# The last MLP block's first product in Strassen form, its weight sums made by accumulating loads, with a plain product at the seam ahead of it

## The chip, the core and the metric

The kernel runs on one core of a Trainium2 chip. The metric is device time in microseconds (us) of one execution; the median of three runs is given with their extremes. A separate execution was recorded by the profiler, and all readings of the trace come from that one.

The names used below are those of the profile: PE is TensorE (matrix products, PEld its weight loads), DVE is VectorE, ACT is ScalarE, POOL is GpSimd, SP is SyncE, which issues most DMAs.

## The reference, cut to what matters

One layer of a hybrid decoder: forgetting attention and an mLSTM side by side, an output projection with layer norm, then an MLP. The change touches only the MLP, which works on 2048 prompt tokens and 64 sampled ones:

```python
x1 = _layer_norm(DN_ALPHA * x + mix, ln1_g, ln1_b)
hid = jnp.square(jax.nn.relu(x1 @ w1))        # w1: 1024 x 4096
return _layer_norm(DN_ALPHA * x1 + hid @ w2, ln2_g, ln2_b)   # w2: 4096 x 1024
```

All is float32. A product is made on PE from parts: an operand is split into a high part, in a shorter format (fp32r in the profile), and a low part (the rest), and three products stand for one: high·high, high·low, low·high.

## The kernel before

The last phase, `phase_c`, goes through the tokens in four blocks (`CB`): three of 512 tokens, and a fourth of 512 prompt tokens with the 64 sampled ones, so W = 576. In a block the 4096 hidden units are cut into eight steps `p` of 512. Step p makes its hidden values in two halves (`hidden(p, half)`, 256 units each) and then adds their part of the second product (`output(p, …)`) to the rows `ys` of the tokens. The steps are staggered: the first half of step p + 1 is issued ahead of `output(p)`, the second half behind it.

`hidden` loads two pieces of w1 (128 x 1024 values, 512 KB each) into tiles `wr` (`raw`, five buffers), splits each into `wh` on ACT (`split_hi`, L153) and `wl` on DVE (`split_lo`, L156; `piece`, four buffers of each), and multiplies: for 2 groups `f` of 128 units, 2 stretches of 288 tokens and 8 pieces `k` of the sum over 1024, three matmuls each (`mm3`, L162 to L164) on the turned x, `x1h` and `x1l`. Each result leaves its PSUM tile `ph` by ACT, as relu (L1460) and square (L1461), into `hq`.

`output` is already in Strassen's form with Winograd's additions: seven products, in the order `order`, in place of eight (84 matmuls of 512 columns in place of 96), each of sums of `hq` (tile `s`, L1508) and of sums of w2, which were made ahead in DRAM (`dw2`, by `w2_sum`, L1224, on POOL's queue). Its results leave their PSUM tiles `py` by DVE (`add`, L1478). The sampled tokens take a product of their own on both halves of PE (`two_sides`, L169). The last step of the fourth block is a plain product, `plain(7)`.

The turned x of a block is made during the last step of the block before: `x1_load` brings a tile of 128 tokens into `xr` (`landing`, two buffers), `x1_turn` transposes it on PE into a tile `px` or `px2` (L1286) and splits it. During the second and third steps of a block the layer norm of the block before (`normed`, L174 to L183) is called piece by piece from the list `later`. In the third block the sampled attention, which fills gaps through the whole phase (`tick`), comes to its end in step 5; it uses four tiles `S` of 128 x 1024 for its scores and the ring `kT`, which afterwards takes the loads of w2 in the fourth block (`spare`).

The program is written for a scheduler: it lays each engine's instructions in one fixed order, and an engine runs its queue in that order, each instruction waiting for the semaphores it names. `tc.issue_after` holds a load back behind an instruction named. Memory is given out by pools with a fixed number of buffers, so a load also waits until the last reader of its buffer is done.

## Time and profile before

| what | us |
|---|---|
| median of three runs | 3163.31 (3162.18 to 3174.97) |
| the profiled execution | 3159.55 |
| its span in the trace | 3157.6 |
| PE busy in the span | 3088.5 |
| DVE, ACT, POOL busy | 2080.6, 1436.6, 911.5 |

The profiled execution lies 3.8 us below the median. The span is the time from the first to the last instruction of that execution; the sum of the prediction is set against 3159.55. Engines overlap, so their busy times are not to be added. The page names releasers and groups by line numbers of the kernel printed above. The fourth block runs from about 2750 us to the end of the span; the lines on it are read in the prediction.

### The profile page before, as it was taken

To read this page: it belongs to the slowest core of one execution; us is meant where nothing else is said; L and a number is where in the kernel's file an instruction comes from. 1 tells how busy PE (TensorE), PEld (TensorE's weight loads), DVE (VectorE), ACT (ScalarE), POOL (GpSimd) and SP (SyncE) were. 2 spreads that over 40 slices of the span, in tenths; PEclk is the share of its full clock that TensorE was granted. 3 is DMA by queue.
4 is the path that set the end of the run, shared out by engine and by line. 5 is a ranking of instruction groups with operands and counts; after the bars stand their busy time and mean duration, and the time that the engine had idled before them with its cause. 6 is when DMAs were issued, how large, how long until landed. Compare 5 with 4: busy or idle time off the path is not lost.

```text
span 3157.6 us, 53760 instructions
## 1 busy us (share of the span) xinstructions
PE 3088.5 (98%) x19869; PEld 2442.9 (77%) x19869; DVE 2080.6 (66%) x5025; ACT 1436.6 (45%) x2629; POOL 911.5 (29%) x976
## 2 busy tenths in 40 slices
PE   8999999999999999999999999999999999999998
PEld 8997787787766667777777776776777777898886
DVE  6956557465488888544566577665586656867667
ACT  4343244334377777422445444453454443554442
POOL 0121232333433433376333324223334121000000
PEclk9999999999999999999999999999999999999999
DMA  5565675877787865587987878868788766543331
GB/s 191 155 213 180 228 234 189 284 269 243 234 260 202 209 172 134 212 304 261 330 289 280 309 255 335 318 242 315 290 308 328 289 230 215 183 154 141 104 118 64
DMA packets 323294, 731.80 MB, mean 232 GB/s; under 512 B 63032, under 2 KB 153656, under 8 KB 322136
## 3 DMA queue, kind: packets, MB, share of 16 engines
q1 hardware_dynamic: 235688, 412.83, 39.5%
q0 software_dynamic: 83808, 304.91, 27.3%
q10 hardware_dynamic: 3536, 10.62, 0.9%
q8 instruction: 157, 2.57, 0.3%
q14 instruction: 105, 0.86, 0.1%
HBM read 675.67 MB, written 86.12 MB: 241 GB/s over the span
## 4 chain that ended last, share of the span: by engine, by line
PE 84%; DMA 6%; DVE 4%; issue 2%; ACT 2%; POOL 1%; SPq 0%; DVEq 0%; POOLq 0%; ACTq 0%
PE ph L164 7%; PE ph L162 7%; PE ph L163 7%; PE py L162 6%; PE py L164 6%; PE py L163 6%; PE pm L162 6%; PE pm L164 6%; PE pm L163 6%; PE sO L1965 3%; PE po L1090 3%; PE sQ L1852 3%; PE pt L1080 3%; DMA vt<-cache_v,idxV 3%; PE pS L1035 2%
## 5 line engine op out<-in xcount | busy, mean ns | idle before, releaser
L156 DVE TENSOR_TENSOR wl<-wr,wh 128x1024 fp32r<-128x1024 f32 x300 | 365.7, 1221 | 227.9 <-ACT wh L153 226.9
L153 ACT ACTIVATE wh<-wr 128x1024 fp32r<-128x1024 f32 x300 | 315.6, 1055 | 323.3 <-PE ph L163 152.9
L1829 POOL DMA_INDIRECT kT<-cache_k,idxK x256 | 276.4, 1080 | 625.4 <-PE sQ L1852 560.9
L163 PE MATMUL ph<-x1l,wh 128*128 128x512 f32 (+1 forms) x1280 | 452.1, 353 | 1.8 <-DVE x1l L156 1.8
L162 PE MATMUL ph<-x1h,wh 128*128 128x512 f32 (+1 forms) x1280 | 453.4, 355 | 0.3 <-ACT x1h L153 0.3
L164 PE MATMUL ph<-x1h,wl 128*128 128x512 f32 (+1 forms) x1280 | 449.2, 354 | 0.2
L162 PE MATMUL py<-wh,hh 128*128 128x512 f32 x900 | 354.3, 399 | 0.3 <-ACT hh L153 0.2
L163 PE MATMUL py<-wl,hh 128*128 128x512 f32 x900 | 352.3, 393 | 0.0
L164 PE MATMUL py<-wh,hl 128*128 128x512 f32 x900 | 350.4, 393 | 1.6 <-DVE hl L156 1.6
L1478 DVE TENSOR_TENSOR y<-y,py 128x512 f32<-128x512 f32 x410 | 276.1, 681 | 109.7 <-PE py L164 107.2
L1941 POOL DMA_INDIRECT vt<-cache_v,idxV x197 | 209.8, 1065 | 347.9 <-PE sO L1965 272.3
L162 PEld LDWEIGHTS ph<-x1h,wh 128*128 128x128 f32 x1280 | 240.6, 188 | 36.8 <-issue 6.1
L164 PEld LDWEIGHTS ph<-x1h,wl 128*128 128x128 f32 x1280 | 239.9, 188 | 37.3 <-issue 4.5
L163 PEld LDWEIGHTS ph<-x1l,wh 128*128 128x128 f32 x1280 | 240.5, 188 | 36.3 <-issue 3.7
L162 PE MATMUL pm<-xh,whi 128*128 128x512 f32 (+2 forms) x640 | 230.7, 360 | 0.0
L164 PE MATMUL pm<-xh,wlo 128*128 128x512 f32 (+2 forms) x640 | 228.2, 357 | 0.0
L163 PE MATMUL pm<-xl,whi 128*128 128x512 f32 (+2 forms) x640 | 227.3, 355 | 0.0
L162 PE MATMUL pm<-whi,xh 128*128 128x256 f32 (+4 forms) x624 | 202.8, 326 | 8.6 <-ACT whi L153 8.6
L156 DVE TENSOR_TENSOR wlo<-wra,whi 128x1024 fp32r<-128x1024 f32 (+1 forms) x112 | 140.3, 1254 | 105.4 <-ACT whi L153 105.0
L162 PEld LDWEIGHTS py<-wh,hh 128*128 128x128 f32 x900 | 168.8, 189 | 46.8 <-issue 11.8
L164 PEld LDWEIGHTS py<-wh,hl 128*128 128x128 f32 x900 | 169.5, 188 | 41.0 <-issue 3.3
L163 PE MATMUL pm<-wlo,xh 128*128 128x256 f32 (+4 forms) x624 | 200.7, 322 | 0.6 <-DVE wlo L156 0.6
(380 smaller groups left out, 6476.4 us busy)
## 6 DMA issues: line engine op xcount, KB each, us to landing
wr<-w SPq DMA_DIRECT2D x200, 512.0 KB
wra<-w_in SPq DMA_DIRECT2D x104, 512.0 KB
wr<-dw SPq DMA_DIRECT2D x96, 512.0 KB
dw<-w POOLq DMA_DIRECT2D x48, 512.0 KB, 7.6
Rb<-dR SPq DMA_DIRECT2D x128, 128.0 KB
kT<-dw SPq DMA_DIRECT2D x28, 512.0 KB
kT<-w SPq DMA_DIRECT2D x25, 512.0 KB
xn<-xp_t SPq DMA_DIRECT2D x16, 512.0 KB
```

What stands on the lines that cost most here:

```text
L153: last["ACT"] = A.activation(dst, src, AF.Copy, scale=scale)
L156: r = (eng or V).tensor_tensor(dst, src, hi.bitcast(F32), op=OP.subtract)
L162: T.matmul(ps, wh, xh, start=first, stop=False, skip_group_check=shared)
L163: T.matmul(ps, wh, xl, start=False, stop=False, skip_group_check=shared)
L164: last["PE"] = T.matmul(ps, wl, xh, start=False, stop=stop, skip_group_check=shared)
L1080: turned = T.transpose(pt[:, k], sc[i][0][k0 // 8][:, c:c + 128], ident)
L1090: last["PE"] = T.matmul(po[c:c + 64, q0:], z["vn"][:, k], PTs[k // 4][:, k % 4, q0:], start=(k < 2), stop=(k >= nk - 2), skip_group_check= ...
L1478: V.tensor_tensor(y, y, ps, op=op)
L1829: G.indirect_dma_start(out=piece(n), out_offset=None, in_=ck, in_offset=IO(ap=idxK[:, b, j // 2, j % 2:j % 2 + 1], axis=0))
L1852: r = T.matmul(pq[h4 * 32:h4 * 32 + 32, hg].rearrange("p (k c) -> p k c", k=2), z["qb"][:, hd], kv, start=(db == 0), stop=(db == 1), skip_ ...
L1941: vx["last"] = G.indirect_dma_start(out=vt.rearrange("p f c -> p (f c)"), out_offset=None, in_=cv, in_offset=IO(ap=idxV[:, b, (kt % 4) * 4 ...
L1965: after_ = T.matmul(po[r:r + 32], z["PT"][:, hg, 2 * f + g, pg].rearrange("p h q -> p (h q)"), vts[f][:, g, hg * 256:(hg + 1) * 256], star ...
```

## The change

The fourth block's first product takes the form that the second one has. With x1 cut into four quarters (two halves of the tokens, two of the sum over 1024) and w1 likewise, seven products `n` of sums give the four quarters of the result. `hidden_s(p, …)` makes a step's 512 units at once, in the order `H_ORDER` = 1, 6, 7, 4, 5, 3, 2: for each product 2 groups f, 4 pieces k and three matmuls of 288 columns, so 7 x 2 x 4 x 3 = 168 matmuls a step, where there were 192.

The seven operands of x are made once. `last_block` loads the block's four row tiles into memory that the sampled attention has left (`nat`); `operand_sums` makes the sums on POOL, during step 6 of the third block; `operand_turn` transposes and splits each of seven operands of two tiles, and `sampled_turn` does the same for the sampled rows. These turns are spread over the output products of steps 6 and 7 of the third block, in PSUM tiles `side` that the sampled attention has left.

The operands of w1 are made anew in each step, by loads. Four loads bring quarters into tiles for the products 1, 6, 7 and 5, and one each later for 3 and 2; accumulating loads (`more`, on POOL's queue) add a second quarter to 7 and 5, and a second and a third to 6. When the tile of product 6 has been split, a fourth quarter is added to it, and it is split again as product 4's operand. A step so has six plain loads and five accumulating ones of w1, where it had four plain ones. Seven pieces are split where there were four. The signs are taken by the results: ACT copies the results of products 1, 6 and 7 into `hq` tiles (L1599 of the changed kernel), DVE adds or subtracts those of 5, 3 and 2 (L1604), ACT makes relu and square.

At the seam the third block's last second product is plain (`plain`, 96 matmuls of 512 columns for 84), with the turns of the last four operands between its products, and the third block's layer norm is done in two pieces a tile on DVE (`in_two`), with g and b in the memory of `nat`. The four tiles `S` become one tile `S4`, and the two buffers of `xr` one tile of double size; in the fourth block both hold hidden values, operands and the sampled rows' hidden values, which POOL gathers (`gather_sampled`). The loads of w2 in the fourth block take five slots: three of the attention's tiles (`wx`) and, from step 0 on, two of `nat`'s.

Steps are staggered as before, with a difference at the start: `hidden_s(0)` and `hidden_s(1)` stand one behind the other, then `output(0)`, `hidden_s(2)`, `output(1)` and so on; the end is `output(6)` and `plain(7)`.

The core of the diff (`-` before, `+` after):

```diff
-    kx = dict(ring=None, new=False, free=False)
+    kx = dict(ring=None, new=False, free=False, S=ps_.tile([128, 4096], F32, name="S4"))
...
+        xo, nat, diff = {}, {}, kx["S"][:, 1152:2688].rearrange("p (i c) -> p i c", i=3)
+        def last_block():
+            slots.extend([ps_.tile([128, 1024], F32, name="wx", tag=t, bufs=b) for t, b in (("vt", 2), ("vt", 2), ("PTs", 1))])
+            nat[12], nat[13], nat[14], nat[15] = kx["S"][:, 0:1024], slots[0], kx["S"][:, 2688:3712], slots[1]
+            for t in (12, 14, 13, 15):
+                SY.dma_start(nat[t], dx1[t * 128:t * 128 + 128])
+            x = pk_.tile([128, 5, 4, 288], F32R, name="xo5", tag="kT", bufs=1)
+            for i, n in enumerate((5, 6)):
+                xo[n] = [x[:, i * 2], x[:, i * 2 + 1]]
+            xo[3] = [x[:, 4], pcw.tile([128, 4, 288], F32R, name="xo1", tag="xr", bufs=1)]
...
+        def operand_sums(j):
+            xa, xb = nat[12 + j], nat[14 + j]
+            G.tensor_tensor(diff[:, 0], xb[:, 0:512], xb[:, 512:1024], op=OP.subtract)
+            G.tensor_tensor(xb[:, 0:512], xa[:, 0:512], xb[:, 0:512], op=OP.subtract)
+            G.tensor_tensor(diff[:, 1], diff[:, 0], xa[:, 0:512], op=OP.subtract)
+            G.tensor_tensor(diff[:, 2], xa[:, 512:1024], diff[:, 1], op=OP.add)
...
+        def operand_turn(n, j):
+            if n not in xo:
+                x1_pool()
+                x = C["px"].tile([128, 4, 2, 4, 288], F32R, name="xo")
+                for i, m in enumerate((1, 7, 2, 4)):
+                    xo[m] = [x[:, i, 0], x[:, i, 1]]
+            xa, xb = nat[12 + j], nat[14 + j]
+            src = {1: xa[:, 0:512], 2: xa[:, 512:1024], 4: xb[:, 512:1024], 7: xb[:, 0:512],
+                   5: diff[:, 0], 6: diff[:, 1], 3: diff[:, 2]}
+            px = side_bank().rearrange("p (k c) -> p k c", k=4)
+            for k in range(4):
+                T.transpose(px[:, k], src[n][:, k * 128:k * 128 + 128], ident)
+            h, l = (x[:, :, j * 128:j * 128 + 128] for x in xo[n])
+            split_hi(h, px)
+            C["turned"] = split_lo(l, px, h)
...
+            def h_tile():
+                count[0] += 1
+                if ci == 3 and count[0] % 4 == 0:
+                    return kx["S"][:, 1152:2304].rearrange("p (f c) -> p f c", f=2)
+                return ph.tile([128, 2, 576], F32, name="hq", bufs=3)
...
+            def hidden_ops(p):
+                w = lambda q: I["w1"][q % 2 * 8 + p, q // 2]
+                R = {}
+                def load(n, q):
+                    R[n] = raw()
+                    SY.dma_start(R[n], w(q))
+                def more(n, q):
+                    with tc.issue_after(last["POOL"].ins):
+                        last["POOL"] = G.dma_start(R[n], w(q), accum_op=OP.add)
+                for n in (1, 6, 7, 5):
+                    load(n, 0 if n != 7 else 3)
+                for n in (6, 7, 5):
+                    more(n, 1)
+                more(6, 3)
+                load(3, 3)
+                def made(n):
+                    r = piece(None, R[6 if n == 4 else n].rearrange("p (k c) -> p k c", k=4))
+                    if n == 1:
+                        load(2, 2)
+                    elif n == 6:
+                        more(6, 2)
+                    return r
+                return made, {}
+            H_ORDER = (1, 6, 7, 4, 5, 3, 2)
...
+                X = [ppc.tile([128, 512], F32, name="ph", tag="ph", bufs=2)[:, 0:288] for _ in range(2)]
+                Z = None
+                for at_, n in enumerate(H_ORDER):
+                    hidden_made(hp, H_ORDER[:at_ + 3])
+                    wh, wl = hp[1][n]
+                    xh, xl = xo[n]
+                    if n in (5, 2):
+                        Z = [side_bank()[:, 0:288] for _ in range(2)]
+                    for f in range(2):
+                        ps = (X if n in (1, 6, 7, 4) else Z)[f]
+                        c = slice(f * 128, f * 128 + 128)
+                        for k in range(4):
+                            mm3(ps, wh[:, k, c], wl[:, k, c], xh[:, k], xl[:, k], n in (1, 5, 2) and k == 0, n in (4, 3, 2) and k == 3, True)
+                        if n in (1, 6, 7):
+                            A.copy(part({1: 0, 6: 1, 7: 3}[n], f), ps)
+                        elif n == 4:
+                            A.activation(part(2, f), ps, AF.Relu)
+                        else:
+                            o = part({5: 3, 3: 1, 2: 0}[n], f)
+                            V.tensor_tensor(o, ps, o, op=OP.add if n == 2 else OP.subtract)
+                        if f == 1 and n in (4, 5, 3, 2):
+                            o = whole({4: 2, 5: 3, 3: 1, 2: 0}[n])
+                            if n != 4:
+                                A.activation(o, o, AF.Relu)
+                            A.activation(o, o, AF.Square)
+                    if n == 2:
+                        gather_sampled(p)
+                    if later:
+                        later.pop(0)()
+                    hooks.pop(at_, lambda: None)()
...
+            if ci == 3:
+                hp = {0: C.pop("hs")}
+                def begin(p):
+                    hp[p] = hidden_ops(p)
+                ops_of = lambda p, *ns: lambda: pre.append(ahead(p, *ns))
+                pre = []
+                hidden_s(0, hp.pop(0), {5: lambda: begin(1), 6: lambda: hidden_made(hp[1])})
+                for p in range(7):
+                    hidden_s(p + 1, hp.pop(p + 1), {5: lambda: begin(p + 2) if p < 6 else None, 6: ops_of(p, *order[:2])})
+                    if p == 0:
+                        slots.extend(C["gb"])
+                    output(p, pre.pop(), [], {5: early if p == 6 else lambda: hidden_made(hp[p + 2])})
+                plain(7, [(i, half) for i in range(4) for half in range(2)], [], {})
+                break
...
+                elif p == 6 and ci == 2:
+                    operand_sums(0)
+                    for n in (5, 6, 3):
+                        turns += [lambda: None, lambda: None, lambda: None, lambda n=n: operand_turn(n, 0)]
+                    turns.append(lambda: operand_sums(1))
+                elif p == 7:
+                    turns = [lambda n=n, j=j: operand_turn(n, j) for n in (1, 7, 4, 2) for j in range(2)]
+                    turns.insert(2, sampled_turn)
...
+                    if p == 7 and ci == 2:
+                        plain(p, [(i, half) for half in range(2) for i in range(4)], turns,
+                              {4: lambda: hidden_made(C["hs"], H_ORDER[:1]), 6: lambda: hidden_made(C["hs"])})
+                        while turns:
+                            turns.pop(0)()
+                    else:
+                        output(p, pre[0], turns, {})
```

Three places show how the order of instructions moves. A row names line, operation, output and inputs with the shape, and behind it the semaphores that it waits for. First PE, in a step in the middle of the fourth block. Before, two ph tiles (the two stretches of 288 tokens) take the first product in turns, with x1h and x1l as the moving operand; here they go from w1's first piece (wl_29395) to its second (wh_29400), and then to an output product:

```order
L164 MATMUL ph_29432<-x1h_28138,wl_29395 128x288
L162 MATMUL ph_29405<-x1h_28138,wh_29400 128x288 [waits Activation_49]
L163 MATMUL ph_29405<-x1l_28139,wh_29400 128x288
L162 MATMUL ph_29432<-x1h_28138,wh_29400 128x288
L162 MATMUL py_29227<-wh_29316,hh_29311 128x512 [waits DVE_49]
L163 MATMUL py_29227<-wl_29317,hh_29311 128x512
L164 MATMUL py_29227<-wh_29316,hl_29312 128x512
```

After, PE goes from product 7 (wh_29944, with `xo_28155`) to product 5 (wh_30004, in a `side` tile) and back to the second group of product 7; the row on py_29765 is of the output of the step before:

```order
L163 MATMUL py_29765<-wl_29884,hh_29878 128x512
L164 MATMUL py_29765<-wh_29883,hl_29879 128x512
L164 MATMUL ph_29942<-xo_28155,wl_29945 128x288
L162 MATMUL ph_29942<-xo_28155,wh_29944 128x288
L163 MATMUL ph_29942<-xo_28155,wh_29944 128x288
L164 MATMUL ph_29942<-xo_28155,wl_29945 128x288
L162 MATMUL side_30069<-xo5_27718,wh_30004 128x288 [waits Activation_49]
L163 MATMUL side_30069<-xo5_27718,wh_30004 128x288
L162 MATMUL ph_29943<-xo_28155,wh_29944 128x288 [waits Activation_49]
```

What was a run of one product, broken by output products, is now an interleaving of products of the same step, and PE waits for ACT at the first use of product 5's weights and at the second ph tile.

Then ACT, in a step in the middle of the fourth block. Before, it splits the pieces of w1 (wr) as they come and drains ph as relu and square:

```order
L153 ACTIVATE hh_29581<-hq_29096 128x512 [waits DVE_49,PE_49,Activation_49]
L153 ACTIVATE wh_29394<-wr_29392 128x1024 [waits PE_49,Activation_49]
L153 ACTIVATE wh_29400<-wr_29398 128x1024 [waits DMAHW6_49,PE_49]
L1460 ACTIVATE hq_29404<-ph_29405 128x288 [waits DVE_49,PE_49,Activation_49]
L1461 ACTIVATE hq_29404<-hq_29404 128x288 [waits Activation_49]
L153 ACTIVATE wh_29515<-wr_29513 128x1024 [waits DMAHW7_49,PE_49]
L1460 ACTIVATE hq_29404<-ph_29432 128x288 [waits PE_49]
L1461 ACTIVATE hq_29404<-hq_29404 128x288 [waits Activation_49]
L153 ACTIVATE wh_29521<-wr_29519 128x1024 [waits DMAHW0_49,DVE_49,PE_49]
```

After, in a like place: wh_29921 is product 6's weights; the tile wr_29698 that it reads is read a second time by wh_29974, product 4's, behind the add that the semaphore DMASW1 reports; wh_30004 is product 5's, and the copies drain products 1 and 6:

```order
L153 ACTIVATE wh_29921<-wr_29698 128x1024 [waits DMASW0_49,PE_49]
L1599 COPY hq_29940<-ph_29942 128x288 [waits DVE_49,PE_49,Pool_49]
L153 ACTIVATE wh_29944<-wr_29700 128x1024 [waits DMASW6_49,DVE_49,PE_49]
L1599 COPY hq_29940<-ph_29943 128x288 [waits PE_49]
L1599 COPY hq_29941<-ph_29942 128x288 [waits PE_49]
L153 ACTIVATE hh_30197<-s_30173 128x512 [waits PE_49]
L153 ACTIVATE wh_29974<-wr_29698 128x1024 [waits DMASW1_49,PE_49]
L153 ACTIVATE wh_30004<-wr_29702 128x1024 [waits DMASW7_49,DVE_49,PE_49]
L1599 COPY hq_29941<-ph_29943 128x288 [waits PE_49]
L153 ACTIVATE wh_30034<-wr_29708 128x1024 [waits DMAHW2_49,PE_49]
L1599 COPY hq_29941<-ph_29942 128x288 [waits PE_49]
```

The second split of wr_29698 stands between the drains of product 6's two groups, and product 5's split and the drain of ph_29943 stand behind it.

Last POOL, at the beginning of the fourth block. Before, it has only the small operations of the layer norm there, and no DMA:

```order
L191 TENSOR_TENSOR ln_r2_27739<-ln_r2_27739,nhalf_74 64x1 [waits DVE_49]
L179 TENSOR_TENSOR ln_rs_28425<-ln_rs_28425,nhalf_74 128x1 [waits DVE_49,Activation_49]
L179 TENSOR_TENSOR ln_rs_28492<-ln_rs_28492,nhalf_74 128x1 [waits DVE_49,Activation_49]
L179 TENSOR_TENSOR ln_rs_28572<-ln_rs_28572,nhalf_74 128x1 [waits DVE_49,Activation_49]
L179 TENSOR_TENSOR ln_rs_28639<-ln_rs_28639,nhalf_74 128x1 [waits DVE_49,Activation_49]
L191 TENSOR_TENSOR ln_r2_31717<-ln_r2_31717,nhalf_74 64x1 [waits DVE_49]
```

After, the five adds of step 0 (wr_28053 is product 6's tile, wr_28055 product 7's, wr_28057 product 5's), between the layer norm's rows, and the first of step 1:

```order
L1551 DMA wr_28053<-w1 128x1024 [waits DMAHW4_49,DMAHW5_49,DMAHW3_49,DMAHW6_49,DMAHW2_49,DMAHW7_49,DMAHW1_49,DVE_49]
L1551 DMA wr_28055<-w1 128x1024 [waits DMAHW5_49,DMAHW4_49,DMAHW7_49,DMAHW2_49,DVE_49]
L1551 DMA wr_28057<-w1 128x1024 [waits DMAHW5_49,DMAHW0_49,DVE_49]
L1551 DMA wr_28053<-w1 128x1024 [waits DMASW1_49]
L1823 TENSOR_TENSOR ln_r3_28355<-ln_r3_28355,nhalf_74 128x1 [waits DVE_49]
L1823 TENSOR_TENSOR ln_r3_28358<-ln_r3_28358,nhalf_74 128x1 [waits DVE_49]
L1551 DMA wr_28053<-w1 128x1024 [waits DMASW4_49,DVE_49,Activation_49]
L1823 TENSOR_TENSOR ln_r3_28361<-ln_r3_28361,nhalf_74 128x1 [waits DVE_49]
L1823 TENSOR_TENSOR ln_r3_28364<-ln_r3_28364,nhalf_74 128x1 [waits DVE_49]
L1551 DMA wr_28580<-w1 128x1024 [waits DMASW6_49,DMAHW5_49,DMASW5_49,DVE_49]
```

The third add to wr_28053 waits for DVE and ACT, which split what the tile held; step 1's adds stand behind it in POOL's queue.

More of the change, by code (lines that the diff above doesn't have):

```diff
@@ L1278, in x1_turn @@
         if i == 0 and 0 in halves:
-            if t == 12:
-                x1_pool()
-            C["x"] = [C["px"].tile([128, 8, 576 if t == 12 else 512], F32R, name=m, bufs=1) for m in ("x1h", "x1l")]
+            C["x"] = [C["px"].tile([128, 8, 512], F32R, name=m, bufs=1) for m in ("x1h", "x1l")]
         xh, xl = C["x"]
@@ L1628, in early @@
-            def early():
-                for q in (0, 2):
-                    lastw[q] = weight(I["w2"][7, q])
+                if W > 512:
+                    hs = sampled_of.pop(p)
+                    for half in range(2):
+                        ps = ppc.tile([128, 512], F32, name="ph", tag="ph", bufs=2)
+                        for k in range(2):
+                            two_sides(ps, [(hs[n][:, k], lastr[n * 2 + half][:, k]) for n in range(2)], k == 0, k == 1)
+                        for n in range(2):
+                            add(16, half, ps[n * 64:n * 64 + 64])
@@ new lines, in plain @@
+                for at_, (i, half) in enumerate(loops):
+                    r, c = i // 2, slice(i % 2 * 128, i % 2 * 128 + 128)
+                    ps = ppc.tile([128, 512], F32, name="py", bufs=4)
+                    for n in range(2):
+                        (h, l), (wh, wl) = x[r, n], lastw[n * 2 + half]
+                        for k in range(2):
+                            mm3(ps, h[:, k, c], l[:, k, c], wh[:, k], wl[:, k], n == k == 0, n == k == 1, True)
+                    add(blk[i], half, ps)
+                    if turns:
+                        turns.pop(0)()
+                    hooks.pop(at_, lambda: None)()
@@ L1671, in phase_c @@
                         tick(100.0)
+                if p == 6 and ci == 2:
+                    later = [lambda: (operand_turn(5, 1), operand_turn(6, 1)), lambda: operand_turn(3, 1)]
                 if p < 7:
-                    hidden(p + 1, 1, {(2, 5): sampled, (3, 6): early}.get((ci, p)))
+                    hidden(p + 1, 1, {(2, 5): sampled, (2, 6): early}.get((ci, p)))
+                if p == 5 and ci == 2:
+                    last_block()
         es.close()
```

148 lines of the change are left out of this document (101 added, 47 removed).

## The prediction

> **What bounds the kernel now.** I read the page first: its engine line, where TensorE (PE) is busy nearly throughout, then the fourth block by equal windows.
>
> ```profile
> span 3157.6 us, 53760 instructions
> PE 3088.5 (98%) x19869; PEld 2442.9 (77%) x19869; DVE 2080.6 (66%) x5025; ACT 1436.6 (45%) x2629; POOL 911.5 (29%) x976
> ```
>
> A 98% busy PE says that PE's own work sets the time, but a mean hides stages. The change touches the fourth MLP block and the seam ahead of it. In the chain of waits the sampled tokens' group "PE ph L169 x16" comes once for each eighth of the hidden units (I call it a step, p), so its starts give the period.
>
> ```profile
> 2736.03 0.87 PE px L1286 x8
> 2796.72 3.58 PE ph L169 x16
> 2845.44 3.58 PE ph L169 x16
> ```
>
> The period is 2845.44 − 2796.72 = 48.72 us. Cut at these starts, the windows read (length, busy time of each engine with its instructions, clock, DMA share, GB/s):
>
> ```profile
> core 0: us, PE busy (x) PEld busy (x) DVE busy (x) ACT busy (x) POOL busy (x), PEclk, DMA share, GB/s
> 2796.72:2845.44 48.72, 48.69 (x295) 42.22 (x296) 32.02 (x43) 21.90 (x35) 0.00 (x0) 1.00 0.33 119
> 2991.62:3040.34 48.72, 48.69 (x294) 42.23 (x296) 32.01 (x43) 21.89 (x35) 0.00 (x0) 1.00 0.34 120
> ```
>
> PE has no gap, its granted clock is full, DVE stands at 32.0/48.7 = 66%, ACT at 45%, POOL does nothing, and DMA has two thirds free. The waits of PE from 2700 to 3143 us, in full:
>
> ```profile
> PE py L164 <- DVE hl L156: 0.8, 1, 0.8
> PE px L1286 <- DVE x1l L156: 0.3, 1, 0.3
> PE py L162 <- ACT hh L153: 0.2, 1, 0.2
> ```
>
> So in this block time is the number of matmuls times their pitch, and a matmul less is time less, as long as the others keep up. The pitch (start to start) is taken from PE's timeline, since the busy time of one (0.29 or 0.39 us) overlaps the next.
>
> ```profile
> 2801.04 0.40 PE L163 MATMUL py<-wl,hh 128*128 128x512 f32 x1
> 2803.09 0.39 PE L164 MATMUL py<-wh,hl 128*128 128x512 f32 x1
> ...
> 2858.21 0.29 PE L162 MATMUL ph<-x1h,wh 128*128 128x288 f32 x1
> 2859.93 0.29 PE L162 MATMUL ph<-x1h,wh 128*128 128x288 f32 x1
> ```
>
> The first two are the first and last of ten successive starts: 2.05/9 = 0.228 us for 512 columns. The other two are the first and last of fourteen: 1.72/13 = 0.1323 us for 288. Check: 192 × 0.1323 + 84 × 0.228 + 3.58 = 48.1 of 48.72 us.
>
> **The change, part by part.**
>
> *Fewer matmuls.* A step's first product falls from 2 × 2 × 8 × 3 = 192 matmuls of 288 columns to 7 × 2 × 4 × 3 = 168. Over eight steps: 8 × 24 × 0.1323 = **−25.4 us**.
>
> *Plain product at the seam.* The third block's last second product goes from 84 to 96 matmuls of 512 columns: 12 × 0.228 = **+2.7 us**.
>
> *Turning the operands.* Before, block 4's x took 4 × 8 + 8 = 40 transposes; now 14 × 4 + 8 = 64. Eight take 0.87 us (the px row), so 24 × 0.109 = **+2.6 us**. PE's net is −20.1 us.
>
> *Sums of x on POOL.* Eight operations 128x512, priced by the nearest row:
>
> ```profile
> L747 POOL TENSOR_TENSOR Wq<-Wq,qk 128x512 f32<-128x512 f32 x16 | 22.1, 1381 | 0.0
> ```
>
> 8 × 1.38 = 11 us, in two halves, beside PE's output products of the third block's step 6; the first turn of each half stands some products behind it. I take 0; at worst one half is caught up with, 4 × 1.38 = 5.5 us.
>
> *More drains and splits.* Per step three more pieces of w1 are split, and six drains of 288 columns go to DVE.
>
> ```profile
> L153 ACT ACTIVATE wh<-wr 128x1024 fp32r<-128x1024 f32 x24 | 25.4, 1057 | 27.0 <-PE py L164 27.0
> L156 DVE TENSOR_TENSOR wl<-wr,wh 128x1024 fp32r<-128x1024 f32 x24 | 29.3, 1222 | 4.9 <-ACT wh L153 4.9
> L1478 DVE TENSOR_TENSOR y<-y,py 128x512 f32<-128x512 f32 x79 | 53.5, 682 | 35.6 <-PE py L164 35.5
> L1460 ACT ACTIVATE hq<-ph 128x288 f32<-128x288 f32 x48 | 19.4, 404 | 66.3 <-PE ph L164 66.3
> L1461 ACT ACTIVATE hq<-hq 128x288 f32<-128x288 f32 x48 | 21.2, 443 | 1.3
> ```
>
> DVE: 32.0 + 3 × 1.22 + 6 × (0.40 to 0.68; I take 0.45, by 288 being nearer to ACT's row of that width) = 38.4 us (40 at the upper end). ACT: 3 × 1.06 more, and its drains go from 8 × 0.85 = 6.8 us to eight of 0.40 and seven passes over 576 elements of about 0.7: 8.1 us; together 26.4. The new period of PE is 48.72 − 24 × 0.1323 = 45.5 us, so DVE is at 84%, ACT at 58%. Neither is the bound by its sum; PE's buffers (two ph, two side, four py) must cover DVE's order. Cost between 0 and 0.5 us a step, by half a DVE split that a drain stands behind; I take 0.2 × 7 = **+1.4**.
>
> *Sums of w1 by accumulating loads.* This is the uncertain term. Per step 18 transfers of 512 KB replace 11, which makes 119 × 18/11 × 48.7/45.5 = 208 GB/s and a DMA share of about 0.58. Block 4 shows no accumulating load. The nearest are the w2 sums in DRAM, earlier, by the same POOL queue:
>
> ```profile
> dw<-w POOLq DMA_DIRECT2D x48, 512.0 KB, 7.6
> dw<-dw POOLq DMA_DIRECT2D x16, 512.0 KB, 5.4
> ```
>
> The second are plain copies, sixteen of the first too, so an add costs some 2 us. Landing hangs on the load of the queues; issues from 1200 to 1245 us (all accumulating) and from 1170 to 1200 (all plain), each with its window:
>
> ```profile
> DMA to landing us min/median/max: 5.7/6.8/10.1
> 1200.00:1245.00 45.00, 44.72 (x318) 31.89 (x316) 34.72 (x142) 34.14 (x81) 15.28 (x23) 1.00 0.71 149
> ...
> DMA to landing us min/median/max: 3.9/5.0/5.9
> 1170.00:1200.00 30.00, 29.34 (x208) 20.39 (x207) 25.40 (x107) 24.26 (x56) 14.56 (x24) 1.00 0.61 179
> ```
>
> At a share of 0.58 I take the landing L as 5.7 us: below the 6.8 by the lighter load. Bounds: 3.9 (the fastest plain copy) to 10.1.
>
> The Trainium skill, DMA: Bandwidth & Descriptors, section "Anatomy of one DMA — SWDGE (gpsimd) path", fits a POOL-issued transfer as 2.0 us plus bytes over 436 GB/s, an estimate of 3.2 us for 512 KB; no row here is that fast, and the accumulating ones take twice that. By it the term below would be near 1 us, which is the first rival.
>
> Where L bites: of a step's five adds only one is tight. The tile of product 6 is split, then the fourth matrix is added to it, and the sum is split as product 4's operand. ACT holds that split in order ahead of product 5's split and of product 6's second drain, so all three stand behind the landing. In the steady order, from the start of product 6, PE has 24 + 12 matmuls of 288 and 18 of 512 columns before it needs product 5's weights: 36 × 0.1323 + 18 × 0.228 = 8.9 us; less two splits on ACT, 2 × 1.06, **the slack is 6.8 us**. L = 5.7 fits; above it each step loses L − 6.8.
>
> The first two steps run without output products between them. From the issue in step 0 (0.3 us after product 1 begins) PE has about 34 matmuls of 288 columns and eight transposes: 4.5 + 0.9 − 0.3 − 2.1 = 3.0 us of slack. In step 1 product 5's weights are wanted 36 matmuls after product 6 begins, and its split is itself only just ready (half a us late): 4.8 − 0.5 − 2.1 = 2.2. At L = 5.7 these lose 2.7 + 3.5 = 6.2 us; bounds 0.9 + 1.7 = 2.6 (L = 3.9) and 7.1 + 7.9 = 15 (L = 10.1). I add 0.8 for step 1's chain, whose adds stand on POOL behind step 0's: **+7.0**. Ahead of the block, product 6's tile takes its load only when the seam's plain product has split its second weights, by the order some 18 us of PE work before its own split is due; a load and two adds are 5.0 + 2 × 5.7 = 16.4 us, so 0 (2 us at L = 7). Nothing else queued on SP or POOL there is wanted sooner.
>
> *The end.* The last product is the same; at the end DVE, not PE, closes it:
>
> ```profile
> 3131.00:3144.00 13.00, 13.00 (x59) 10.75 (x58) 12.67 (x26) 0.00 (x0) 2.38 (x2) 1.00 0.20 61
> 3144.00:3158.00 14.00, 2.38 (x11) 1.64 (x9) 10.57 (x21) 0.00 (x0) 2.77 (x3) 0.67 0.29 113
> ```
>
> DVE is 12.7 of 13 us busy there and on for 10.6 us after PE, with the sampled rows' norm in it; that norm now falls before the plain loop's own drains, so some of it is off the end: 0 to −3, taken **−1**.
>
> *Sum.* −20.1 + 1.4 + 7.0 − 1 = **−12.7 us**. It stands against the profiled execution (3159.55 us around a span of 3157.6); the median of the three runs, 3163.31, is 3.8 higher, and the same sum put to it gives **3151 us**.
>
> **The rivals.**
>
> *No stall.* If L is near 4 the adds vanish behind PE's work and DVE's order costs nothing: −20.1 − 1 + about 1 = −20, so 3143. For it: PE waited 1.3 us in all over this block, DMA has room, 3.9 us has been seen. Against: no accumulating load was under 5.7. Chance 0.30.
>
> *The adds come late (slower).* One mechanism: the add for product 4, with ACT's queue held behind it, in all eight steps. It decides from L = 6.8. At 8 the seven later steps lose 8.4 and the first two 10.8: −20.1 + 1.4 + 19.2 + 0.8 − 1 = 0, so 3163. At 10.1 they lose 23 and 15: −20.1 + 1.4 + 38 + 0.8 − 1 = +19, so 3182, slower. For it: half of the dw<-w rows took 7.6 or more, and ACT and DVE must answer each landing at once. Against: the share here is below those windows', and the destination is read by nothing else then. Chance 0.15 over +0.5%, 0.10 for 3157 to 3179.
>
> *DVE becomes the bound.* It is 84% busy in a fixed order; if drains of ph and side stand behind splits that wait for landings, PE loses 1 us a step: 8 × 1 = 8 against −12.7, so 3158. For it: DVE's idle is 7 us a step only. Against: before, at 66%, PE lost nothing. Chance 0.10, within 0.5%.
>
> *The change doesn't shorten PE's stream.* Excluded as far as the matmuls go: the order lists 168 of them a step.
>
> **How the numbers follow.** The forecast case (3146 to 3157) has 0.35, no stall 0.30, DVE 0.10, late adds 0.25 in two parts. A measurement of this kernel tells about 0.5% (15.8 us) from no change: faster is below 3147.5, slower above 3179. Faster: the no-stall case and a fifth of the forecast, 0.37; slower: 0.15; same: 0.48. The range leaves out 0.2: it goes from 3139 (no stall, with the end's full −3) to 3176, nearly the price at L = 10.1, which is the upper bound of the unknown term.
>
> **What would show it.** Period of the chain's L169 groups in the fourth block: 45.5 us if only matmuls count, 45.5 + (L − 6.8) if adds come late. PE's waits in the first 30 us of the block: about 6 us, on ACT's split or drain (L153, L1599), the same with L near 3 gone. The landing of the new POOL loads, by their row: 5.7 right, 4 the first rival, 8 and more the second. DVE by step 38 us. Wrong would be: waits of PE on DVE drains in every step, or a longer third block.

## The result and the profile after

The changed kernel takes 3184.62 us (median of nine runs, 3180.94 to 3190.7) against 3163.31 us: a ratio of 1.0067, with a 95% interval of 1.0054 to 1.0080. It is slower by 21 us, where 12 us faster was forecast. The profiled execution took 3186.24 us; its page begins:

```profile
span 3184.5 us, 53752 instructions
PE 3086.5 (97%) x19713; PEld 2430.0 (76%) x19713; DVE 2120.4 (67%) x5092; ACT 1458.2 (46%) x2648; POOL 962.2 (30%) x1040
```

The steady part of the fourth block came out as computed. The chain of waits gives the period, from the sampled tokens' first group of one step to that of the next, and the windows give one step (columns as before):

```profile
2932.94 1.87 PE ph L169 x8
...
2978.94 1.87 PE ph L169 x8
```

```profile
2932.94:2978.94 46.00, 45.97 (x270) 38.98 (x272) 37.48 (x51) 25.16 (x37) 5.89 (x7) 1.00 0.75 205
```

A step takes 46.00 us where it took 48.72. So the loss lies elsewhere, and the way to find it is to set the same instruction of both traces side by side and read the difference of their starts:

| from, to | before | after | difference |
|---|---|---|---|
| start, first matmul of the sampled tokens' projection (`ys`) | 2657.0 | 2672.6 | +15.6 |
| that, first matmul of 288 columns | 95.8 | 98.6 | +2.8 |
| that, last matmul of the program | 393.2 | 401.2 | +8.0 |
| that, end | 11.6 | 12.2 | +0.6 |

Of the 15.6 us, 1.4 are there by 2315 us; the rest arises inside the third block, which the prediction took as untouched. And the fourth block, forecast 17 us shorter, is 8 us longer. Its beginning shows why. The stretches from `ys` to the block's start, the block's first 113 us, the rest to the last matmuls, and the tail:

```profile
2672.60:2774.00 101.40, 101.40 (x504) 79.88 (x504) 76.58 (x120) 43.66 (x66) 12.92 (x13) 1.00 0.52 154
2774.00:2886.93 112.93, 91.24 (x557) 81.25 (x557) 71.25 (x89) 50.46 (x77) 14.29 (x19) 0.92 0.77 222
2886.93:3170.00 283.07, 282.90 (x1578) 233.72 (x1578) 234.54 (x323) 143.44 (x204) 31.01 (x38) 1.00 0.62 173
3170.00:3184.50 14.50, 2.74 (x13) 1.93 (x11) 11.29 (x22) 0.00 (x0) 1.84 (x2) 0.72 0.37 145
```

In the second row PE is idle for 112.93 − 91.24 = 21.7 us, and its granted clock is 0.92. The clock is at one half in two stretches there:

```profile
2780.49:2787.32 6.83, 4.62 (x19) 4.62 (x20) 5.59 (x5) 3.16 (x5) 0.00 (x0) 0.50 0.44 163
2811.21:2821.45 10.24, 4.66 (x18) 4.38 (x19) 2.93 (x3) 2.92 (x4) 0.85 (x1) 0.50 0.39 82
```

PE works for 4.62 and 4.66 us of them and is idle in the rest, so half of 9.28, or 4.6 us, is lost beside the idle time. PE's waits in the block's first part (2750 to 2900 us):

```profile
PE ph L162 <- ACT wh L153: 10.7, 2, 10.0
PE side L162 <- ACT wh L153: 7.5, 2, 5.7
PE ph L164 <- DVE wl L156: 1.6, 1, 1.6
PE py L163 <- DVE wl L156: 1.4, 1, 1.4
PE ph L162 <- ACT S L1599: 0.4, 1, 0.4
```

Behind ACT's splits stand the adds. ACT's timeline, where the bracket is the idle time before a row and what ended it:

```profile
2780.64 2.00 ACT L153 ACTIVATE wh<-wr 128x1024 fp32r<-128x1024 f32 x2 [6.04 <-DMA wr<-w]
...
2815.68 2.00 ACT L153 ACTIVATE wh<-wr 128x1024 fp32r<-128x1024 f32 x2 [6.15 <-DMA wr<-w]
```

The first is the tight add of step 0, product 4's. The second is product 6's in step 1, and POOL's timeline has its story: the two adds of product 6 are the first row and the last of the pair, those of products 7 and 5 stand between.

```profile
2788.16 0.88 POOL L1551 DMA_DIRECT2D wr<-w  x1 [13.08 <-DVE y L1826]
2798.26 0.85 POOL L1551 DMA_DIRECT2D wr<-w  x1 [9.21 <-DVE wl L156]
2802.37 1.73 POOL L1551 DMA_DIRECT2D wr<-w  x2 [3.27 <-DVE hq L1604]
```

The time from issue to landing, of the pair in the last row, and then of all forty adds:

```profile
DMA to landing us min/median/max: 9.5/11.1/12.7
```

```profile
DMA to landing us min/median/max: 5.4/8.4/14.2
```

Product 6's first add is issued at 2788.2 and takes 9.3 us, so its second could go at 2797.5. It goes at 2802.9, behind two adds that wait for their own loads, and lands 12.7 us later, at 2815.7. That is where the 10.0 us wait comes from: 5.4 us of it by the place in POOL's queue, the rest by landings of 9.3 and 12.7 us and a first add that itself goes late.

### The profile page after: what moved, and what is told of

Read it like the earlier page. It is cut to its first block, busy times and chain, and to the rows that moved or that the text cites. A ratio compares the mean times of both kernels' runs of the same rounds, so it can differ in the third digit from the quotient of the medians.

```text
span 3184.5 us, 53752 instructions
## 1 busy us (share of the span) xinstructions
PE 3086.5 (97%) x19713; PEld 2430.0 (76%) x19713; DVE 2120.4 (67%) x5092; ACT 1458.2 (46%) x2648; POOL 962.2 (30%) x1040
## 5 line engine op out<-in xcount | busy, mean ns | idle before, releaser
L156 DVE TENSOR_TENSOR wl<-wr,wh 128x1024 fp32r<-128x1024 f32 x321 | 392.3, 1226 | 252.4 <-ACT wh L153 247.9
L153 ACT ACTIVATE wh<-wr 128x1024 fp32r<-128x1024 f32 x321 | 336.7, 1055 | 344.3 <-PE ph L163 183.0
L162 PE MATMUL ph<-x1h,wh 128*128 128x512 f32 x768 | 305.2, 397 | 0.2 <-ACT x1h L153 0.2
L163 PE MATMUL ph<-x1l,wh 128*128 128x512 f32 x768 | 302.8, 394 | 1.8 <-DVE x1l L156 1.8
L164 PE MATMUL ph<-x1h,wl 128*128 128x512 f32 x768 | 301.4, 395 | 0.0
L164 PE MATMUL pm<-whi,xl 128*128 128x256 f32 (+4 forms) x624 | 199.6, 320 | 0.2 <-DVE xl L156 0.2
L163 PEld LDWEIGHTS py<-wl,hh 128*128 128x128 f32 x904 | 171.0, 189 | 36.7 <-issue 2.1
L1064 ACT ACTIVATE S<-S,mx 128x1024 f32<-128x1024 f32 (+2 forms) x192 | 171.7, 897 | 45.8 <-DVE mx L1050 45.5
```

The lines of the kernel that those rows point to most:

```text
L153: last["ACT"] = A.activation(dst, src, AF.Copy, scale=scale)
L156: r = (eng or V).tensor_tensor(dst, src, hi.bitcast(F32), op=OP.subtract)
L162: T.matmul(ps, wh, xh, start=first, stop=False, skip_group_check=shared)
L163: T.matmul(ps, wh, xl, start=False, stop=False, skip_group_check=shared)
L164: last["PE"] = T.matmul(ps, wl, xh, start=False, stop=stop, skip_group_check=shared)
L1064: last["ACT"] = A.activation(sp[:, :w], sp[:, :w], AF.Exp, bias=mx[:, 7:8], accum_out=lp[:, k:k + 1])
```

## The experiments

They ran on four chips, where the kernel before took 3202.5, 3201.4, 3161.4 and 3162.6 us (e1, e2, e3, e5; e4, e6 to e8; e9, e10; e11). Each ratio is to the kernel before on the same chip. The changed kernel itself gave 1.0067 and, as e4, 1.0085, so ratios of different chips compare to about 0.2% only. The block's time is that of one trace, from its first 288-column matmul to the last matmul. e3 and e5 leave sums of w1 out and serve the timing alone.

| run | ratio, 95% interval | fourth block, us |
|---|---|---|
| before | 1 | 393.2 |
| changed | 1.0067, 1.0054 to 1.0080 | 401.2 |
| e1 early loads back | 1.0035, 1.0021 to 1.0050 | 402.2 |
| e2 before, loads late | 1.0024, 1.0003 to 1.0046 | 393.2 |
| e3 no adds, steps 0, 1 | 1.0009, 0.9998 to 1.0021 | 383.9 |
| e4 changed, again | 1.0085, 1.0064 to 1.0106 | 400.1 |
| e5 adds as plain loads | 1.0027, 1.0011 to 1.0042 | 387.2 |
| e6 adds reordered | 1.0041, 1.0027 to 1.0054 | 392.4 |
| e7 = e6 + e1 | 1.0031, 1.0014 to 1.0047 | 392.7 |
| e8 sums in DRAM + e1 | 1.0019, 1.0002 to 1.0035 | 382.9 |
| e9 = e6, product 4 late | 1.0059, 1.0044 to 1.0075 | 398.5 |
| e10 = e9 + e1 | 1.0039, 1.0026 to 1.0052 | 396.9 |
| e11 sums at the start + e1 | 1.0037, 1.0020 to 1.0053 | 384.7 |

### The third block: two loads that are gone

Before the change, the loads of block 4's first two tiles of x were laid by the scheduler at the front of the third block, since their buffers were free. The change loads x later and elsewhere. With the two loads gone, PE's order differs from that point on: groups of the sampled attention (`sO`) stand some matmuls sooner. Counted in matmuls of the two products (`ph`, `py`) from the block's first transpose, the group that was behind the 252nd is now behind the 228th, and that behind the 358th now behind the 332nd. PE then waits for gathers that land when they landed before (83 and 85 us after the block's first transpose before, 82 and 85 after). PE's waits for them from 2300 to 2500 us, before (first row) and after:

```profile
PE sO L1965 <- DMA vt<-cache_v,idxV: 3.8, 3, 1.8
```

```profile
PE sO L2196 <- DMA vt<-cache_v,idxV: 8.2, 3, 4.5
```

and the stretch behind the longest of them, before and after, where the changed kernel's clock is 0.79:

```profile
2400.00:2420.00 20.00, 20.00 (x107) 15.25 (x100) 14.71 (x22) 6.89 (x10) 5.68 (x4) 1.00 1.01 397
```

```profile
2400.00:2420.00 20.00, 19.01 (x93) 13.36 (x86) 11.97 (x18) 6.87 (x11) 3.79 (x4) 0.79 0.93 362
```

From the first split of the block's turned x to `ys`, before and after, PE is idle for 5.0 and 11.6 us, and busy for 7.6 us more at the lower clock; together these are the 14.2 us:

```profile
2316.80:2657.00 340.20, 335.20 (x2082) 250.63 (x2080) 225.63 (x398) 152.78 (x239) 99.65 (x90) 1.00 0.78 280
```

```profile
2318.20:2672.60 354.40, 342.77 (x2082) 255.58 (x2080) 226.78 (x398) 152.83 (x239) 101.32 (x94) 0.97 0.77 274
```

**e1** puts two such loads back:

```diff
                 if p == 5 and ci == 2:
+                    for t in (12, 13):
+                        x1_load(t)
                     last_block()
```

> The changed kernel, with two loads of block 4's rows into the landing tile put back (nobody reads them), at the end of the third block's step 5; the order then brings them to the front of the third block, as before the change, and PE's order there is that of before. Theory: some 10 us of the loss came about in the third block, since without these two loads the order puts groups of the sampled attention some us earlier on PE than their gathers of v land, and each such wait is followed by a stretch at half the granted clock. It expects 3172 to 3177 us, PE's waits for vt between 2300 and 2500 us down from 8.2 to about 4, and a granted clock of 1.00 from 2400 to 2420 (0.79 in the changed kernel). Rival, that the gathers were late by chance in that execution: 3182 to 3187 us.

Measured: 1.0035. The attention's groups there are back behind the 252nd and 358th matmul, and between 2300 and 2550 us its trace has a single wait for vt, of 0.9 us; the stretch from 2420 to 2440 us (this chip is some 30 us later there) has the full clock.

**e2** does the reverse to the kernel before:

```diff
-                    begun = [x1_load(t) for t in CB[ci + 1][:2]]
+                    begun = []
+                    for t in CB[ci + 1][:2]:
+                        x = landing()
+                        if ci == 2:
+                            G.tensor_copy(x[:1, :1], ys[8][:1, :1])
+                        SY.dma_start(x, dx1[tok_r(t):tok_r(t) + 128])
+                        begun.append(x)
```

> The kernel of before, with its two early loads of block 4's rows held back behind the third block's step 6 (a one-element copy on POOL into each landing tile, which waits for that step's rows); PE's order in the third block up to its last attention groups becomes that of the changed kernel. Theory: 3163 + about 9 = 3170 to 3175 us, with waits of PE for vt of about 8 us near 2400 us and a dip of the granted clock behind them. Rival, that the order of the third block costs nothing: 3160 to 3166 us.

Measured: 1.0024, 7.7 us, with a wide interval. The groups stand behind the 228th and 332nd matmul, as in the changed kernel, and the kernel before now has waits and a dip. Its waits for vt from 2400 to 2500 us (4.8 us, where some 8 were expected), and then the stretch with the dip:

```profile
PE sO L1971 <- DMA vt<-cache_v,idxV: 4.8, 2, 2.9
```

```profile
2420.00:2440.00 20.00, 15.24 (x93) 9.85 (x93) 8.11 (x19) 6.76 (x11) 6.81 (x7) 0.75 1.03 418
```

Both ways agree, and so do all traces: from the first split of the block's turned x to `ys`, the seven kernels with the loads late (the changed one, e2 to e6, e9) take 353 to 358 us, and the six with the loads early (the one before, e1, e7, e8, e10, e11) 340 to 351. The pairs e4 and e1, e6 and e7, e9 and e10 differ by 10, 5 and 6 us there. So the order costs some 5 to 10 us; by their ratios alone the last two pairs, whose intervals overlap, would not show it. A further 1 to 6 us around 2650 us stands in the traces with `last_block`; it was not taken apart.

### The start of the fourth block: the adds

**e3** leaves the adds out of the first two steps, **e5** makes all adds plain loads:

```diff
                 def more(n, q):
+                    if p < 2:
+                        return
                     with tc.issue_after(last["POOL"].ins):
...
-                        last["POOL"] = G.dma_start(R[n], w(q), accum_op=OP.add)
+                        last["POOL"] = G.dma_start(R[n], w(q))
```

> The changed kernel without the accumulating loads of steps 0 and 1 of the fourth block, which leaves those sums of w1 out; everything else stands. Theory: the start of the block lost 21 us in waits of PE behind the adds' landings and 8 us more at half clock; it expects 3155 to 3161 us, PE's waits on wh between 2770 and 2870 us under 3, and a granted clock of 1.00 there. Rival, that ACT and DVE would hold PE there anyway (splits and drains of two steps without output products between them): 3172 us or more.

> The changed kernel with its accumulating loads made plain loads, on the same queue, to the same tiles, in the same order and with the same waits, which leaves the sums of w1 out. It tells the cost of adding from the cost of waiting for a second transfer: if adding itself is slow, the landing falls from a median of 8.4 to about 6 us and the time by 6 to 10 us, to 3175 to 3179; if the load of the queues and the chain of transfers set it, the landing stays above 7.5 and the time within 4 us of 3184.6.

Measured, e3: 1.0009, by the ratios 18 us below the changed kernel and 24 below e4, where the theory gave 24 to 30; the block falls to 383.9 us, some 16 us below that of the same kernel with its adds. The waits in its first part are DVE's now:

```profile
PE ph L164 <- DVE wl L156: 4.6, 2, 2.7
PE py L162 <- DVE y L1628: 1.7, 1, 1.7
PE py L163 <- DVE wl L156: 1.1, 1, 1.1
```

So the rival had a part: with the adds gone, PE still waits 7.4 us for DVE. e5: 1.0027, the block at 387.2 us. With the chain of transfers, its queue and its waits kept, over half of the loss goes when the transfers don't add, more than either expectation had it; one wait of 6.2 us for a split of w1 stays. This chip's traces show no landings for these transfers, but the time that POOL's queue took of the 16 DMA engines, for the same bytes in the same window, shows why. First e1, whose transfers add, then e5 (packets, MB, share):

```profile
q0 software_dynamic: 5760, 20.97, 22.2%
```

```profile
q0 software_dynamic: 5760, 20.97, 11.7%
```

A transfer that adds occupies the DMA engines nearly twice as long as a plain one.

**e4** repeats the changed kernel, **e6** puts each step's adds in the order of need, **e7** adds e1:

```diff
-                for n in (1, 6, 7, 5):
+                for n in (6, 1, 7, 5):
                     load(n, 0 if n != 7 else 3)
-                for n in (6, 7, 5):
-                    more(n, 1)
-                more(6, 3)
+                for n, q in ((6, 1), (6, 3), (7, 1), (5, 1)):
+                    more(n, q)
```

> The changed kernel itself, beside the kernel before on the chip of the runs below, so that they have a measure of their own: earlier 1.0067 of before. Expected within 1.005 to 1.0085; PE waits of some 6 and 10 us on wh at the start of the fourth block.

> The changed kernel with each step's loads of w1 in the order 6, 1, 7, 5 (it was 1, 6, 7, 5) and its adds in the order 6, 6, 7, 5 (it was 6, 7, 5, 6). Theory: PE's 10 us wait in step 1 is product 6's chain, whose load stands behind product 1's on SP and whose second add stands on POOL behind the adds of 7 and 5, which wait for their own loads; with the new order the chain ends 8 to 12 us sooner, the wait falls under 3 us and the half clock behind it goes: 3184.6 - 12 = 3170 to 3176, or 0.25 to 0.45% below the changed kernel. Rival, that the wait comes from the load of the queues (landings of 9 to 13 us while some five transfers run): the wait stays over 6 us and the time within 0.15% of the changed kernel.

> The adds reordered as in the run above, and the two early loads of block 4's rows put back as in the first run of all. Theory, that the two losses are apart and add up: 0.32 + 0.25 to 0.45% below the changed kernel, so 0.999 to 1.001 of the kernel before. Rival, that one of them hid part of the other: over 1.002.

Measured: e4 1.0085; e6 1.0041, 0.44% less on the same chip. PE's waits in the block's first part, e4 and then e6:

```profile
PE ph L162 <- ACT wh L153: 10.4, 2, 9.6
PE side L162 <- ACT wh L153: 6.1, 2, 4.4
```

```profile
PE side L162 <- ACT wh L153: 8.1, 2, 4.4
PE ph L164 <- DVE wl L156: 2.0, 1, 2.0
...
PE ph L162 <- ACT wh L153: 0.7, 1, 0.7
```

The wait of 9.6 us is gone and product 4's two adds are left: the order of the queues made the long wait, not their load alone. e6 changes the order on SP and on POOL at once; their shares weren't tried apart. e7 gave 1.0031, which is its rival's side. In its trace the early loads give 5 us in the third block, half of what they gave in e1, and the fourth block stays at 392.7 us; whether the two gains add up in full, the intervals are too wide to say.

**e9** moves product 4 behind products 5 and 3, **e10** adds e1:

```diff
-            H_ORDER = (1, 6, 7, 4, 5, 3, 2)
+            H_ORDER = (1, 6, 7, 5, 3, 4, 2)
```

> The reordered adds again, and product 4 moved behind products 5 and 3 (order 1, 6, 7, 5, 3, 4, 2), so that the add whose landing holds ACT has two products more, 48 matmuls or 6.4 us, of cover. Theory: what is left of PE's waits at the start of the block with reordered adds (8.1 us on product 5's weights, behind product 4's in ACT's queue) is that landing; they fall under 2 us, the stretch from 2740 to 2950 us shortens by a further 6 to 10 us, and the time is 0.2 to 0.4% below that run (1.0041): 1.000 to 1.002. Rival, that DVE's splits and drains hold PE there next: waits on DVE of 5 us and more, 1.003 or over.

> The run above with the two early loads of block 4's rows put back. By the stages of the traces the early loads gave 7 to 12 us in the third block (2334 to 2568 us) and the reordered adds 8 at the start of the fourth, while the 16 extra transfers of sums in DRAM lost 10 where they were made; here nothing is lost elsewhere. Theory: 0.25 to 0.35% below the run above, 0.997 to 0.999 of the kernel before. Rival, that the time found in the third block is lost again at the seam: within 0.1% of the run above.

Measured: 1.0059 and 1.0039. e9 is no better than e6 (the ratios overlap, and the block takes 398.5 us where it took 392.4), and the rival holds. From the block's start to 3170 us, e9 waits:

```profile
PE ph L164 <- DVE wl L156: 10.2, 7, 1.9
PE ph L162 <- ACT hq L1600: 9.4, 1, 9.4
```

Each of seven steps now waits some 1.5 us for a split on DVE, and the wait at the start only changed its name. ACT's timeline shows what holds the drain:

```profile
2796.19 1.06 ACT L153 ACTIVATE wh<-wr 128x1024 fp32r<-128x1024 f32 x1 [10.68 <-DMA wr<-w]
2797.16 0.39 ACT L1600 ACTIVATE hq<-ph 128x288 f32<-128x288 f32 x1
```

It stands behind a split whose tile takes two adds, one behind the other: the first is issued at 2780.3 us and takes 6.1, the second goes at 2786.7 and takes 9.4. By this chain, and by its place in the order, the split is step 1's product 6 again. e10 is 6 us better than e9 in the third block, where e1 gained 10.

**e8** and **e11** make the sums of steps 0 and 1 ahead, in DRAM, by 16 transfers; these are e8's loads and the order of its sums (tile, quarter or the tile before, add):

```diff
+    W1_SUMS = ((0, 0, False), (3, 3, False), (0, 1, True), (3, 1, True), (1, None, False), (1, 3, True), (2, None, False), (2, 2, True))
...
+                    dsum = {5: 0, 6: 1, 4: 2, 7: 3}
+                        SY.dma_start(R[n], dw1[p, dsum[n]] if n in dsum else I["w1"][q % 2 * 8 + p, q // 2])
```

> The changed kernel with the two early loads of block 4's rows put back, and with the w1 sums of steps 0 and 1 made ahead in DRAM, by 16 more transfers beside those that make w2's sums, so that these two steps have seven plain loads and no adds. Theory: both losses go as far as the runs before showed (0.32 and 0.58%), so 0.997 to 0.999 of the kernel before; PE's waits in the first 100 us of the block under 8 us, on DVE. Rival, that the 16 transfers cost as much where they are made (900 to 1300 us, where DMA is 70 to 80% busy): 1.000 or more, with the time already lost at 1300 us.

> As the run with the sums of steps 0 and 1 in DRAM and the two early loads of block 4's rows, with the order 1, 6, 7, 4, 5, 3, 2 of the changed kernel, but with those 16 transfers issued at the beginning of the program (behind the gathers of logf, some 30 us in), where POOL is idle for 70 us. In the earlier run the stretch from 908 to 1318 us was 10.4 us longer with them, and the start of the fourth block 17.2 us shorter. Theory: POOL is part of the loop that sets that stretch, and at the beginning it is not, so the 10 us are not paid: 0.3% below that run's 1.0019, 0.997 to 1.000 of the kernel before, and nothing lost against the changed kernel by 300 us. Rival, that the transfers cost their time wherever they are made, by the load on the queues: 5 us or more late by 300 us, and 1.001 or over.

Measured: 1.0019 and 1.0037. The block falls to 382.9 and 384.7 us, as without adds, but the sums cost their gain where they are made: 10.4 us between 908 and 1318 us in e8, 16 us within the first 110 us in e11. The first 150 us, the changed kernel and then e11:

```profile
0.00:150.00 150.00, 140.09 (x1082) 137.48 (x1083) 116.18 (x360) 57.85 (x116) 12.43 (x22) 1.00 0.54 172
```

```profile
0.00:150.00 150.00, 127.27 (x953) 124.55 (x954) 100.05 (x304) 51.66 (x100) 19.27 (x34) 0.95 0.69 205
```

POOL was idle there, but the DMA queues were not: their share rises from 0.54 to 0.69, 19 loads of w_in are issued in that time where e10, whose beginning is that of the changed kernel, issues 21, and PE has 12.8 us less work done. The rival, that the transfers cost their time wherever they are made, holds for both places. None of the versions beats the kernel before.

## Why the prediction was wrong, point by point

- **Matmuls, turns, plain product: right.** The period is 46.00 us (45.5 computed); the stage with the turns and the plain product grew by 2.8 us, where 2.7 + 2.6 less the 1.4 us that PE idled there before make 3.9. DVE is busy 37.5 us a step (38.4), ACT 25.2 (26.4), the traffic 205 GB/s (208).
- **The slack of the steady steps: right.** The tight adds there land in 5.4 and 5.5 us (5.7 taken), under the slack of 6.8, and PE waits for none after 2870 us. The median of 8.4 is that of all adds, most of them with cover. The DMA share was mis-sized, 0.75 where 0.58 was worked out from bytes: an add takes more of the queues than a load of the same size, by e1 and e5 nearly twice. The late adds' sums also counted seven steps behind the first two, where eight less two are six; with six, 3163 and 3182 us would be 3162 and 3179.
- **The start of the block: the step that failed first.** "I add 0.8 for step 1's chain, whose adds stand on POOL behind step 0's" priced the chain of product 6 as if its second add followed its first. It stood behind the adds of products 7 and 5, and landed in 12.7 us: 10.0 us of waiting. The prediction read the order of POOL's rows and the landing times, but not when the adds ahead in the queue could themselves be issued. e6 shows that the order of the queues, SP's and POOL's together, was the cause. The tight adds lost 7.5 us where 6.2 was forecast, but the nearness is luck: it is 5.7 + 1.8 where 2.7 + 3.5 was priced, since step 0's add took some 7.9 us from its issue to its split, and step 1's 5.6.
- **The third block: the step that failed second.** "Before, block 4's x took 4 × 8 + 8 = 40 transposes" counted the work that moved, but not that its two loads left the place in SP's order where the scheduler had put them, and with them the order of the attention. e1, e2 and the traces show some 5 to 10 us. The text looked for "a longer third block" only as a sign of being wrong; it had no term for it.
- **Waits priced at their length.** Every wait of the sum was taken at its own length. In the trace some waits of a few us are followed by matmuls at half speed (shown in the last section). PE was busy for 31.7 us at half the clock before and for 55.4 after: half the difference, 12 us, of the 27 by which the two profiled executions differ.

The sum with these in place: −20.1 for PE's work, some +3.5 for the period's 0.5 us in the seven steps, +21.7 of waits and +4.6 of clock in the block's first part, +14 in the third block make +24, where the spans differ by 26.9. Of the rest, 1.4 are there by 2315 us, 0.6 lie behind the last matmul (−1 was forecast), and about 1 was not taken apart. The rival that came nearest named the adds, but in the steady steps; it was the start that failed, and that its 3182 us lies near the measured time is luck.

## What to carry to other kernels

Where a change moves or drops a load, compare the whole order from there on, not only the place of the change: a scheduler's order far ahead of it can shift and lay an engine's work before its data. Transfers that build on each other belong in one queue in the order of need, each priced with what stands ahead of it there; work that is cheap in the steady state is dearest at the start, where nothing covers it. Work taken off a busy place comes back where it is put: 16 transfers cost 10 us beside those of w2's sums, and 16 us at the beginning, which looked free by POOL's idle time.

## What the runs showed of the hardware

A wait of PE can cost more than its length. PE's timeline in the changed kernel around the 5.70 us wait, where each row is one matmul and the rows left out have the same pitch:

```profile
2782.70 0.61 PE L162 MATMUL side<-xo,wh 128*128 128x288 f32 x1 [5.70 <-ACT wh L153]
...
2785.98 0.44 PE L162 MATMUL ph<-xo,wh 128*128 128x288 f32 x1
2786.22 0.44 PE L163 MATMUL ph<-xo,wh 128*128 128x288 f32 x1
...
2787.51 0.29 PE L163 MATMUL ph<-xo,wh 128*128 128x288 f32 x1
2787.64 0.30 PE L164 MATMUL ph<-xo,wl 128*128 128x288 f32 x1
```

The pitch is 0.24 us behind the wait and 0.13 from 2787.4 us on. The Trainium skill, TensorE: Matmul & The Clock Gate, section "HAM oscillation — how this bites in real kernels", gives the rule "no PE-idle gaps >~3.4µs". The trace agrees for the waits of 5.70 and 9.98 us, but here shorter ones were followed by the half clock too: in the changed kernel the stretch with two waits of 0.9 and 1.6 us has

```profile
2640.00:2660.00 20.00, 17.58 (x88) 12.22 (x87) 7.67 (x12) 6.51 (x10) 3.20 (x3) 0.83 0.68 242
```

a clock of 0.83, 3.4 us lost behind 2.4 us of waiting. Not every such pair does it: in the kernel before, waits of 1.8 and 1.4 us at 2347 to 2349 us left the clock alone:

```profile
2340.00:2360.00 20.00, 16.80 (x122) 11.67 (x115) 15.56 (x36) 6.29 (x9) 9.96 (x10) 1.00 1.03 411
```

Up to the last matmul, every stretch at the half clock lasted 3.41, 6.83 or 10.24 us in these two traces, and it can begin while PE still waits: the one here begins at 2780.49 us, 2.2 us ahead of the wait's end. That the waits cause the dips was read from their places, and not tried apart.
